# Block 1 of the tokens gathered in place of block 5, with its first rows fetched in the front

## The chip, the cores and the metric

The kernel runs on one core of one Trainium2 chip. The metric is the device time of one execution in microseconds (us), median of several runs. The engines are TensorE (PE; its weight loads are listed apart as PEld), VectorE (DVE), ScalarE (ACT), GpSimd (POOL), and SyncE (SP), which issues plain DMAs. POOL issues the indirect DMAs.

## What is computed

One layer of a streaming encoder on 1024 tokens of width 1024, in float32: an adaptive norm, latent attention and a recurrent branch, merged and projected onto the residual stream; then a second norm and a mixture of 16384 tiny experts. The last part is what the change touches:

```
q = (xt @ w_query).reshape(TOKEN_BLOCK, PEER_HEADS, 2, PEER_HALF)
s = einsum('thpd,hpnd->thpn', q, sub_keys)
s_top, i_top = top_k(s, 16)
cand = s_top[:, :, 0, :, None] + s_top[:, :, 1, None, :]
best, pos = top_k(cand, 16)
idx = ...
g = softmax(best)
act = gelu(einsum('td,thkd->thk', xt, expert_u[idx]))
out = einsum('thk,thkd->td', g * act, expert_v[idx])
```

Each token chooses 8 x 16 = 128 experts out of 16384. An expert is a row of `expert_u` and a row of `expert_v`, of 4 KB each.

## The kernel before

The tokens are eight blocks of 128. The experts of a block are computed in one of two ways. A **gathered** block (`GATHER`, line 23: 0, 5, 6, 7) fetches its own rows: 128 indirect DMAs of 128 rows (512 KB) from `expert_u`, each multiplied with the tokens and summed by one DVE instruction (the dot), then the same number of bytes from `expert_v`, summed by PE with weights from a transposed table. A **dense** block (`DENSE`, the other four: 512 tokens) runs through all experts by matrix products, with a table G that says which of the products count.

The kernel has two halves.

**The front** works through the tokens in two parts of 512 (`part`, line 483): attention, first merge with the projections `ps_ga` and `ps_pa` (`merge_a`), recurrence (`lru`), second merge (`merge_b`), output projection, norm and queries (`ffn_in`, line 839). After part 0's queries, `after_part` (line 1099) puts the expert work of part 0 as a list of small steps into `self.steps`, and while part 1 runs, `pump` (line 137) pops a number of these steps at fixed places. The rates (line 97, second number of each pair: 2 per attention unit, 2.9 per weight product, 6.6 and 3.3 in `ffn_in`) say how many. So the order of the work on each engine is this program order, written out by the counter. What is left over at the end, and part 1's own steps, run behind the last query.

The steps are of four kinds:

- routing of a block (`route`, line 963): DVE picks the 16 best pairs of each head, the weights and the expert numbers. For a gathered block, a further step `turn` transposes the numbers with PE. The routing's tiles `ra`, `rb`, `rc` have one buffer each.
- first rows of a block (`gather_u`, line 1112). In the front it works in rounds of `GUF` = 3: a step `dots` (line 1151) runs three dots on DVE (line 1154) and then issues the next three fetches on POOL (line 1146) into the three buffers that it has just read.
- second rows of block 0 (`sooner_v`, line 1195): a step issues four indirect DMAs of half rows on POOL (line 1209) and lets PE add up the four fetched one step earlier (line 1222). There are 64 row steps, with four buffers of 1024 elements, two for each step.
- the table of a dense block (`table`, line 1263): 32 quads of four tokens, each with two DVE instructions (lines 1294 and 1295), six products on PE (1284, 1286, 1302) and two copies by ACT (1310) into a staging pair `gs`. The pair is written to DRAM after four quads (line 1314); there are two staging buffers, both in use for each four quads.

Before the change, the list of part 0 is block 0's routing, then block 0's rows (first and second) merged evenly with the routing and tables of blocks 1, 2 and 3. Part 1's list is block 4's routing and table, the table merged with the routing of block 5 (`BRIDGE`), whose numbers and weights are kept in constant buffers so that its gathers can begin with the dense stage.

**The dense stage** (`dense`, line 1331) takes the 128 slabs of 128 experts in turn. For each slab: load of `uT` (512 KB, SP) and its split into two fp32r halves by ACT and DVE, 24 matmuls into `ps_A` (`first`), gelu, multiplication with G (`weigh`, from `Gt`, 1 MB for every four slabs), load and split of `expert_v`; after every four slabs, 4 x 2 groups of 12 matmuls into `ps_y` (`second`). A point is 24 matmuls, either of `first` or of one block in `second`; behind each point the same counter pops steps, at a rate of list length over 248 points (128 + 32 x 4, times 0.97). The list of the dense stage is: first rows of block 5 merged with the routings of 6 and 7 and with 40 empty steps; first rows of 6 merged with second rows of 5; first rows of 7 with second rows of 6; second rows of 7. A step there issues one gather (line 1128 for first rows, line 1174 for second rows), runs one dot (line 1134), or adds up four fetched tiles on PE (line 1188).

Of the kernel before, what the change touches and what calls it, by code (L numbers as in the profile page):

```python
# [19 lines left out]
NT = S // T  # L20
EPS = 1e-6
NEG = -3.0e38
GATHER = (0, 5, 6, 7)
SOONER = (0,)
BRIDGE = 5
LATER = (6, 7)
DENSE = tuple(b for b in range(S // 128) if b not in GATHER)
TD = 128 * len(DENSE)
# [56 lines left out]
class Builder:  # L85
    def __init__(self, ctx, tc, I, out, dbg=None, stop=None):
# [6 lines left out]
        self.steps = []  # L93
        self.blocks = {tb: dict(tb=tb) for tb in GATHER}
        self.rate = dict(unit=(1, 2), w=(1.5, 2.9), z=(4, 6.6), q=(2, 3.3))
# [743 lines left out]
    def ffn_in(self, p, ys):  # L839
# [41 lines left out]

        gb = [i for i in range(4) if p * 4 + i in GATHER]

# [79 lines left out]
    def route(self, tb):  # L963

        nc = self.nc
        late = tb in LATER
# [80 lines left out]
        def end():  # L1047
            W2 = t["W"].rearrange("p a b -> p (a b)")
            if f"E{tb}" in self.dbg:
                ee = t["a"]  # L1050
                nc.vector.scalar_tensor_tensor(ee, t["ij"][:, 0, :], 128.0, t["ij"][:, 1, :], op0=ALU.mult, op1=ALU.add)
                self.show(f"E{tb}", ee.rearrange("p (a b) -> p a b", a=8))
                self.show(f"W{tb}", t["W"])
            if tb in GATHER:
                g = self.blocks[tb]
                for n, dt in (("w", F32), ("ei", I32)):
                    g[n] = self.cp.tile([128, 128], dt, name=f"{n}{tb}") if tb == BRIDGE else \
                        (self.gp if late else self.fp).tile([128, 128], dt, tag="g_" + n, bufs=1, name="g_" + n)
                if tb not in SOONER:
                    g["eT"] = self.kept(g, [128, 128], I32, "eT")  # L1060
                nc.vector.tensor_copy(g["w"], W2)
                E = t["ij"][:, 0, :]
                nc.vector.scalar_tensor_tensor(E, E, 128.0, t["ij"][:, 1, :], op0=ALU.mult, op1=ALU.add)
                nc.vector.tensor_copy(g["ei"], E)
                g["E"] = E
            else:
                self.chosen = t["ij"], W2

        def turn():
            g = self.blocks[tb]  # L1070
            pt = self.psum([128, 128], "ps_eT")
            nc.tensor.transpose(pt, g.pop("E"), self.ident)
            if tb in SOONER:
                g["eh"] = [self.fp.tile([128, 128], I32, tag="g_eh", bufs=2, name="g_eh") for _ in range(2)]
                for hf in range(2):
                    nc.vector.tensor_scalar(g["eh"][hf], pt, 2.0, float(hf), op0=ALU.mult, op1=ALU.add)
            else:
                nc.vector.tensor_copy(g["eT"], pt)
# [8 lines left out]
    def kept(self, g, shape, dt, name):  # L1087

        tb = g["tb"]
        if tb in SOONER:  # L1090
            return self.fp.tile(shape, dt, tag="g_" + name, bufs=1, name="g_" + name)
        return self.cp.tile(shape, dt, name=f"{name}{tb}") if name == "eT" and tb == BRIDGE else \
            self.gp.tile(shape, dt, tag="g_" + name, bufs=3 if name == "wT" else 2, name="g_" + name)

    def routed(self, tb):
        st, turn = self.route(tb)
# [2 lines left out]
    def after_part(self, p):  # L1099

        tbs = [tb for tb in range(p * 4, p * 4 + 4) if tb not in LATER]
        tbs = [tb for tb in tbs if tb in GATHER] + [tb for tb in tbs if tb in DENSE]
        rt = {tb: self.soon.pop(tb) if tb in self.soon else self.routed(tb) for tb in tbs}
        dense = sum([rt[tb] + self.table(tb) for tb in tbs if tb in DENSE], [])
        if p == 0:
            self.steps += rt[0] + self.merge(self.gather_u(self.blocks[0]) + self.sooner_v(self.blocks[0]), dense)
        else:
            n = len(rt[4])
            self.steps += dense[:n + 1] + self.merge(dense[n + 1:], rt[BRIDGE])


    def gather_u(self, g):
# [338 lines left out]
    def run(self):  # L1451
# [28 lines left out]
        with (tc.tile_pool(name="dense_b", bufs=1, reuse_waits="tile") as db,  # L1480
              tc.tile_pool(name="dense_a", bufs=1, reuse_waits="tile") as da,
              tc.tile_pool(name="gather", bufs=1, reuse_waits="tile") as self.gp,
              tc.tile_pool(name="pg", bufs=1, space=bass.MemoryType.PSUM, reuse_waits="tile") as self.pg,
              tc.tile_pool(name="psd", bufs=6, space=bass.MemoryType.PSUM, reuse_waits="tile") as self.ps):
            self.fast = 0
            routes = sum([self.routed(tb) for tb in LATER], [])
            us = {tb: self.gather_u(self.blocks[tb]) for tb in GATHER if tb not in SOONER}
            vs = {tb: self.gather_v(self.blocks[tb]) for tb in GATHER if tb not in SOONER}
            idle = [lambda: None]
            self.steps += self.merge(us[5], routes + idle * 40) + self.merge(us[6], vs[5]) + self.merge(us[7], vs[6]) + vs[7]  # L1490
            self.dense(da, db)
            self.pump(1 << 30)

# [54 lines left out]
```

## Time and profile before

| what | value |
|---|---|
| median of 3 runs | 3584.61 us (3577.67 to 3598.39) |
| the profiled execution's own time | 3616.83 us |
| its span, first to last instruction | 3615.1 us |
| mean granted TensorE clock | 0.942 of full speed |
| busy: PE, DVE, POOL, ACT | 3196.5, 2326.8, 1375.2, 1192.0 us |
| moved by DMA | 915.68 MB, 253 GB/s in the mean |

All rows below come from the one profiled execution. A matmul's record begins before the one in front of it has ended, so PE's busy time is the union of its records. The idle time before an instruction is put down to what released it last. Times are counted from the first instruction.

### The profile page before, as it was taken

What the parts mean: (1) busy time and instruction counts of PE and PEld (TensorE: products, weight loads), DVE (VectorE), ACT (ScalarE), POOL (GpSimd) and SP (SyncE); (2) the same over time, 40 slices, a digit from 0 to 9 for tenths busy, and PEclk for the clock granted to TensorE, in tenths of its full rate; (3) what the DMA queues carried; (4) which work ended last, traced back from release to release, by engine and by line L of the source; (5) the groups of instructions that cost most, each with busy time, mean ns of one, the idle gap of its engine ahead of it and who ended that gap; (6) DMA issues with size and microseconds to landing.
All of it is one profiled execution on the core that took longest, in us unless ns stands there. A gap on an engine that the chain in (4) does not pass through costs nothing.

```text
span 3615.1 us, 43218 instructions
## 1 busy us (share of the span) xinstructions
PE 3196.5 (88%) x15408; PEld 2320.3 (64%) x15408; DVE 2326.8 (64%) x5465; ACT 1192.0 (33%) x1860; POOL 1375.2 (38%) x1180
## 2 busy tenths in 40 slices
PE   6899989587878998897697899998989988899997
PEld 4477778465655665565476776665767666666665
DVE  5535557988778644678788776665666565664334
ACT  4437444266425631333332222222222121222121
POOL 0000013134445456431144445555545555554440
PEclk8899999888999999998898999999999999999998
DMA  8422445166776676763788889998999999898995
GB/s 312 161 81 94 135 138 160 58 211 223 265 264 202 230 250 204 242 201 112 247 266 265 288 278 346 340 372 316 351 331 354 344 335 329 312 350 307 346 326 186
DMA packets 392144, 915.68 MB, mean 253 GB/s; under 512 B 162148, under 2 KB 180708, under 8 KB 388088
## 3 DMA queue, kind: packets, MB, share of 16 engines
q0 software_dynamic: 149504, 536.94, 41.9%
q1 hardware_dynamic: 242424, 375.97, 31.9%
q8 instruction: 121, 1.98, 0.2%
q14 instruction: 95, 0.78, 0.1%
HBM read 851.70 MB, written 61.10 MB: 252 GB/s over the span
## 4 chain that ended last, share of the span: by engine, by line
PE 37%; DMA 25%; DVE 19%; issue 11%; ACT 4%; POOL 3%; another core or an unknown queue 0%; SPq 0%; DVEq 0%; POOLq 0%; ACTq 0%
DMA raw<-in_uT 9%; DMA g_u<-in_expert_u,g_ei 5%; DMA raw<-in_expert_v 4%; DVE g_u L1134 3%; PE ps_G L1302 2%; PE ps_y L692 2%; DMA g_u<-in_expert_u,ei 2%; PE ps_y L695 2%; PE g_y L1188 2%; PE ps_y L693 2%; PE h_y L1222 2%; DVE v L105 2%; POOL g_u L1146 2%; PE ps_A L692 1%; PE ps_A L693 1%
## 5 line engine op out<-in xcount | busy, mean ns | idle before, releaser
L1134 DVE CUSTOM_DVE_ANT_0 g_u<-g_u,g_h 128x1024 f32<-128x1024 f32 x384 | 463.9, 1221 | 149.1 <-DMA g_u<-in_expert_u,g_ei 112.2
L692 PE MATMUL ps_A<-dh,u 128*128 128x512 f32 x1024 | 433.3, 423 | 100.6 <-ACT u L104 89.7
L692 PE MATMUL ps_y<-v,w 128*128 128x512 f32 x1024 | 412.9, 403 | 36.2 <-ACT w L104 27.1
L693 PE MATMUL ps_A<-dh,u 128*128 128x512 f32 x1024 | 422.7, 413 | 8.0 <-DMA dh<-d_h2T 8.0
L1128 POOL DMA_INDIRECT g_u<-in_expert_u,g_ei x256 | 298.6, 1167 | 309.3 <-issue 100.8
L693 PE MATMUL ps_y<-v,w 128*128 128x512 f32 x1024 | 404.6, 395 | 0.0
L1174 POOL DMA_INDIRECT g_v<-in_expert_v,g_eT x256 | 284.8, 1112 | 255.0 <-PE g_y L1188 101.4
L1209 POOL DMA_INDIRECT h_v<-in_expert_v,g_eh x256 | 273.6, 1069 | 283.1 <-PE h_y L1222 212.8
L105 DVE TENSOR_TENSOR u<-raw,u 128x1024 fp32r<-128x1024 f32 x128 | 156.7, 1224 | 326.9 <-ACT u L104 308.9
L104 ACT CAST u<-raw 128x1024 fp32r<-128x1024 f32 x128 | 134.0, 1047 | 659.7 <-DMA raw<-in_uT 620.3
L692 PEld LDWEIGHTS ps_A<-dh,u 128*128 128x128 f32 x1024 | 206.9, 202 | 198.0 <-ACT u L104 110.9
L1128 POOL DMA_INDIRECT g_u<-in_expert_u,ei x128 | 163.2, 1275 | 341.9 <-DVE oneA L1295 103.7
L104 ACT CAST v<-raw 128x1024 fp32r<-128x1024 f32 x128 | 134.3, 1049 | 451.7 <-PE ps_y L695 252.4
L695 PE MATMUL ps_y<-v,w 128*128 128x512 f32 x1024 | 279.7, 394 | 0.3 <-DVE w L105 0.3
L692 PEld LDWEIGHTS ps_y<-v,w 128*128 128x128 f32 x1024 | 195.2, 191 | 124.4 <-issue 36.9
L105 POOL TENSOR_TENSOR whl<-wraw,whl 128x1024 fp32r<-128x1024 f32 x16 | 40.6, 2539 | 585.5 <-ACT whl L104 585.4
L1146 POOL DMA_INDIRECT g_u<-in_expert_u,g_ei x128 | 152.6, 1192 | 282.4 <-DVE g_act L1154 116.3
L695 PE MATMUL ps_A<-dh,u 128*128 128x512 f32 x1024 | 253.1, 389 | 0.8 <-DVE u L105 0.8
L104 ACT CAST whl<-wraw 128x1024 fp32r<-128x1024 f32 (+2 forms) x152 | 151.1, 995 | 297.1 <-PE ps_pb L695 55.2
L693 PEld LDWEIGHTS ps_A<-dh,u 128*128 128x128 f32 x1024 | 206.9, 202 | 52.8 <-DMA dh<-d_h2T 9.0
L105 DVE TENSOR_TENSOR whl<-wraw,whl 128x1024 fp32r<-128x1024 f32 (+2 forms) x136 | 155.2, 1142 | 116.1 <-ACT whl L104 112.7
L695 PEld LDWEIGHTS ps_y<-v,w 128*128 128x128 f32 x1024 | 194.6, 190 | 46.3 <-DVE w L105 4.0
(375 smaller groups left out, 6818.7 us busy)
## 6 DMA issues: line engine op xcount, KB each, us to landing
raw<-in_uT SPq DMA_DIRECT2D x128, 512.0 KB
raw<-in_expert_v SPq DMA_DIRECT2D x128, 512.0 KB
wraw<-in_w_in SPq DMA_DIRECT2D x64, 512.0 KB
d_G<-gs SPq DMA_DIRECT2D x64, 512.0 KB
Gt<-d_G SPq DMA_DIRECT2D x32, 1024.0 KB
wada<-in_w_ada SPq DMA_DIRECT2D x32, 512.0 KB
wraw<-in_w_query SPq DMA_DIRECT2D x32, 512.0 KB
x<-in_x SPq DMA_DIRECT2D x16, 512.0 KB
```

What stands on the lines that cost most here:

```text
L104: self.nc.scalar.copy(hi, src)
L105: (eng or self.nc.vector).tensor_tensor(lo, src, b32(hi), op=ALU.subtract)
L692: nc.tensor.matmul(ps, lh, rh, start=(n == 0), stop=False)
L693: nc.tensor.matmul(ps, lh, rl, start=False, stop=False)
L695: st = nc.tensor.matmul(ps, ll, rh, start=False, stop=(n == len(terms) - 1))
L1128: st = nc.gpsimd.indirect_dma_start(out=u[:], out_offset=None, in_=I["expert_u"], in_offset=bass.IndirectOffsetOnAxis(ap=g["ei"][:, s:s + ...
L1134: nc.vector.tensor_tensor_reduce(out=u, in0=u, in1=g["h2"], scale=1.0, scalar=0.0, op0=ALU.mult, op1=ALU.add, accum_out=g["act"][:, s:s + 1])
L1146: fetch = lambda s: [nc.gpsimd.indirect_dma_start(out=us.setdefault(k, gp.tile([128, 1024], F32, tag="gu", bufs=GUN, name="g_u"))[:], out_ ...
L1174: st = nc.gpsimd.indirect_dma_start(out=v[:], out_offset=None, in_=I["expert_v"], in_offset=bass.IndirectOffsetOnAxis(ap=g["eT"][:, t:t + ...
L1188: nc.tensor.matmul(g["y"][q * 32:(q + 1) * 32, hf * 512:(hf + 1) * 512], zs[n // 16][:, q, (r % 4) * 32:(r % 4 + 1) * 32], v4[q][:, hf * 5 ...
L1209: nc.gpsimd.indirect_dma_start(out=v[:, m, :], out_offset=None, in_=halves, in_offset=bass.IndirectOffsetOnAxis(ap=g["eh"][hf][:, tok:tok ...
L1222: nc.tensor.matmul(t["y"][q * 32:(q + 1) * 32, :], z[:, q, :], v[q // 2][:, q % 2, :], start=(r == 0), stop=(r == 31), tile_position=(0, q ...
```

## The change

Block 1 becomes a gathered block and block 5 a dense one. Block 1 is in part 0, so its routing and its first rows go into part 0's list, behind block 0's second rows; they use block 0's buffers and rounds of three. Its transposed numbers and weights are kept in constant buffers, and its second rows are fetched in the dense stage, merged with the first rows of block 6. The tables of part 0 are now those of blocks 2 and 3; behind the last queries come the tables of blocks 4 and 5. In the dense stage the routings of blocks 6 and 7 stand alone, each ahead of its block's first rows, and the first rows of block 5 with their 40 empty steps fall away. Rates and buffer counts stay.

```diff
--- before.py
+++ after.py
@@ -20,9 +20,8 @@
 NT = S // T
 EPS = 1e-6
 NEG = -3.0e38
-GATHER = (0, 5, 6, 7)
-SOONER = (0,)
-BRIDGE = 5
+GATHER = (0, 1, 6, 7)
+SOONER = (0, 1)
 LATER = (6, 7)
 DENSE = tuple(b for b in range(S // 128) if b not in GATHER)
 TD = 128 * len(DENSE)
@@ -1054,9 +1053,8 @@
             if tb in GATHER:
                 g = self.blocks[tb]
                 for n, dt in (("w", F32), ("ei", I32)):
-                    g[n] = self.cp.tile([128, 128], dt, name=f"{n}{tb}") if tb == BRIDGE else \
-                        (self.gp if late else self.fp).tile([128, 128], dt, tag="g_" + n, bufs=1, name="g_" + n)
-                if tb not in SOONER:
+                    g[n] = (self.gp if late else self.fp).tile([128, 128], dt, tag="g_" + n, bufs=1, name="g_" + n)
+                if tb:
                     g["eT"] = self.kept(g, [128, 128], I32, "eT")
                 nc.vector.tensor_copy(g["w"], W2)
                 E = t["ij"][:, 0, :]
@@ -1070,7 +1068,7 @@
             g = self.blocks[tb]
             pt = self.psum([128, 128], "ps_eT")
             nc.tensor.transpose(pt, g.pop("E"), self.ident)
-            if tb in SOONER:
+            if tb == 0:
                 g["eh"] = [self.fp.tile([128, 128], I32, tag="g_eh", bufs=2, name="g_eh") for _ in range(2)]
                 for hf in range(2):
                     nc.vector.tensor_scalar(g["eh"][hf], pt, 2.0, float(hf), op0=ALU.mult, op1=ALU.add)
@@ -1087,10 +1085,9 @@
     def kept(self, g, shape, dt, name):
 
         tb = g["tb"]
-        if tb in SOONER:
+        if tb == 0:
             return self.fp.tile(shape, dt, tag="g_" + name, bufs=1, name="g_" + name)
-        return self.cp.tile(shape, dt, name=f"{name}{tb}") if name == "eT" and tb == BRIDGE else \
-            self.gp.tile(shape, dt, tag="g_" + name, bufs=3 if name == "wT" else 2, name="g_" + name)
+        return self.cp.tile(shape, dt, name=f"{name}{tb}") if tb in SOONER else self.gp.tile(shape, dt, tag="g_" + name, bufs=3 if name == "wT" else 2, name="g_" + name)
 
     def routed(self, tb):
         st, turn = self.route(tb)
@@ -1101,12 +1098,14 @@
         tbs = [tb for tb in range(p * 4, p * 4 + 4) if tb not in LATER]
         tbs = [tb for tb in tbs if tb in GATHER] + [tb for tb in tbs if tb in DENSE]
         rt = {tb: self.soon.pop(tb) if tb in self.soon else self.routed(tb) for tb in tbs}
-        dense = sum([rt[tb] + self.table(tb) for tb in tbs if tb in DENSE], [])
+        dense = [rt[tb] + self.table(tb) for tb in tbs if tb in DENSE]
         if p == 0:
-            self.steps += rt[0] + self.merge(self.gather_u(self.blocks[0]) + self.sooner_v(self.blocks[0]), dense)
+            g = self.blocks
+            self.steps += rt[0] + self.merge(self.gather_u(g[0]) + self.sooner_v(g[0]) + rt[1] + self.gather_u(g[1]),
+                                             sum(dense, []))
         else:
             n = len(rt[4])
-            self.steps += dense[:n + 1] + self.merge(dense[n + 1:], rt[BRIDGE])
+            self.steps += rt[4] + self.merge(dense[0][n:], rt[5]) + dense[1][len(rt[5]):]
 
 
     def gather_u(self, g):
@@ -1483,11 +1482,9 @@
               tc.tile_pool(name="pg", bufs=1, space=bass.MemoryType.PSUM, reuse_waits="tile") as self.pg,
               tc.tile_pool(name="psd", bufs=6, space=bass.MemoryType.PSUM, reuse_waits="tile") as self.ps):
             self.fast = 0
-            routes = sum([self.routed(tb) for tb in LATER], [])
-            us = {tb: self.gather_u(self.blocks[tb]) for tb in GATHER if tb not in SOONER}
-            vs = {tb: self.gather_v(self.blocks[tb]) for tb in GATHER if tb not in SOONER}
-            idle = [lambda: None]
-            self.steps += self.merge(us[5], routes + idle * 40) + self.merge(us[6], vs[5]) + self.merge(us[7], vs[6]) + vs[7]
+            us = {tb: self.gather_u(self.blocks[tb]) for tb in LATER}
+            vs = {tb: self.gather_v(self.blocks[tb]) for tb in GATHER if tb}
+            self.steps += self.routed(6) + self.merge(us[6], vs[1]) + self.routed(7) + self.merge(us[7], vs[6]) + vs[7]
             self.dense(da, db)
             self.pump(1 << 30)
```

## Rows read from the trace of the kernel before

**Rows 1.** The page, part 1: busy us, share of the span, instructions.

```profile
PE 3196.5 (88%) x15408; PEld 2320.3 (64%) x15408; DVE 2326.8 (64%) x5465; ACT 1192.0 (33%) x1860; POOL 1375.2 (38%) x1180
```

**Rows 2.** Windows by stage: start:end, us, engines' busy us, PE clock, DMA share, GB/s.

```profile
core 0: us, PE busy (x) PEld busy (x) DVE busy (x) ACT busy (x) POOL busy (x), PEclk, DMA share, GB/s
728.00:932.00 204.00, 175.44 (x982) 123.74 (x981) 167.71 (x457) 132.54 (x279) 82.42 (x71) 0.90 0.70 227
932.00:1055.00 123.00, 102.45 (x457) 76.95 (x456) 87.65 (x143) 35.89 (x59) 49.18 (x42) 0.90 0.79 270
1055.00:1220.00 165.00, 140.22 (x609) 93.98 (x608) 131.01 (x359) 90.09 (x115) 82.21 (x71) 0.95 0.66 215
1220.00:1375.00 155.00, 152.93 (x771) 99.71 (x770) 77.06 (x138) 65.07 (x98) 82.51 (x80) 1.00 0.77 255
1375.00:1522.00 147.00, 128.27 (x736) 83.78 (x735) 79.44 (x186) 34.55 (x53) 80.27 (x75) 0.94 0.68 220
1522.00:1667.00 145.00, 141.06 (x781) 101.42 (x780) 116.63 (x561) 51.37 (x88) 48.81 (x48) 0.99 0.57 190
1667.00:1760.00 93.00, 58.86 (x325) 38.62 (x323) 85.78 (x280) 34.67 (x70) 0.94 (x1) 0.80 0.31 114
1760.00:2165.00 405.00, 340.29 (x1390) 272.73 (x1391) 325.44 (x614) 105.85 (x135) 162.31 (x127) 0.92 0.87 279
2165.00:3265.00 1100.00, 1006.93 (x4651) 725.06 (x4650) 678.05 (x1010) 240.67 (x307) 602.18 (x512) 0.96 0.95 339
3265.00:3545.00 280.00, 279.12 (x1425) 183.04 (x1424) 102.02 (x134) 60.33 (x77) 131.70 (x128) 1.00 0.94 333
3545.00:3615.00 70.00, 49.57 (x224) 38.95 (x223) 30.48 (x34) 8.90 (x12) 0.00 (x0) 0.87 0.40 133
```

**Rows 3.** Waits, 2165 to 3265 us: engine line <- releaser: us, times, longest.

```profile
ACT u L104 <- DMA raw<-in_uT: 417.8, 64, 22.0
```

**Rows 4.** Tile g_u, 727 to 1103 us: ns min/median/max, first and last start.

```profile
L1146 POOL DMA_INDIRECT g_u<-in_expert_u,g_ei x128: 932/938/2462, 727.2 to 1095.0; - x128
L1154 DVE CUSTOM_DVE_ANT_0 g_u<-g_u,g_h x128: 1204/1224/1274, 732.6 to 1100.9; 128x1024 f32<-128x1024 f32 x128
```

**Rows 5.** Timeline of DVE, 1059 to 1085 us: start, us, engine, line, operation [idle].

```profile
1059.39 1.22 DVE L1154 CUSTOM_DVE_ANT_0 g_u<-g_u,g_h 128x1024 f32<-128x1024 f32 x1
...
1065.45 1.23 DVE L1154 CUSTOM_DVE_ANT_0 g_u<-g_u,g_h 128x1024 f32<-128x1024 f32 x1 [2.74 <-DMA g_u<-in_expert_u,g_ei]
...
1067.83 1.22 DVE L1154 CUSTOM_DVE_ANT_0 g_u<-g_u,g_h 128x1024 f32<-128x1024 f32 x1
...
1075.35 1.21 DVE L1154 CUSTOM_DVE_ANT_0 g_u<-g_u,g_h 128x1024 f32<-128x1024 f32 x1
...
1082.04 1.21 DVE L1154 CUSTOM_DVE_ANT_0 g_u<-g_u,g_h 128x1024 f32<-128x1024 f32 x1
```

**Rows 6.** The page's part 5 for block 0's second rows; tile h_v's idle; one window.

```profile
L1209 POOL DMA_INDIRECT h_v<-in_expert_v,g_eh x256 | 273.6, 1069 | 283.1 <-PE h_y L1222 212.8
...
  issue: 30.8, 101
...
1350.00:1400.00 50.00, 47.83 (x262) 30.25 (x261) 22.57 (x45) 10.20 (x14) 33.63 (x33) 1.00 0.76 240
```

**Rows 7.** Lines of DVE, 1690 to 1760 us: the table's two instructions.

```profile
L1295 DVE SCALAR_TENSOR_TENSOR oneA<-ps_d,ch 128x512 f32<-128x512 f32 x32 | 21.9, 683 | 3.5 <-PE ps_d L1286 3.3
L1294 DVE TENSOR_TENSOR oneB<-cst,ch 128x512 f32<-128x512 f32 x32 | 21.7, 678 | 0.0
```

**Rows 8.** Timeline of ACT, 1690 to 1760 us: the copies out of the table's products.

```profile
1706.17 1.03 ACT L1310 COPY gs<-ps_G 128x256 f32<-128x256 f32 x2 [2.31 <-DMA d_G<-gs]
...
1712.78 1.04 ACT L1310 COPY gs<-ps_G 128x256 f32<-128x256 f32 x2 [2.30 <-DMA d_G<-gs]
```

**Rows 9.** Windows of the gathered sums' matmuls on PE (tile g_y).

```profile
2165.00:3265.00 1100.00, 124.86 (x1008) 0.96 0.95 339
3265.00:3545.00 280.00, 66.62 (x512) 1.00 0.94 333
```

## The prediction

> **What bounds the kernel now.** I began with part 1 of the page [rows 1]: PE is busy 88% of the span, but no engine is full throughout, so the bound has to be read by stage. I therefore cut the span into windows, from the start of part 1's attention onward [rows 2]. Everything earlier is the same work after the change. Four things are to be seen there. (i) From 728 to 1667 us, the projections of tokens 512 to 1023 run on PE (85 to 99% busy from 1055 on), and block 0's gathers are mixed in by a counter of steps. (ii) From 1667 to 1760 us, behind the last query, the front's remaining steps run alone: DVE is busy 86 of 93 us, DMA 31%. (iii) The dense stage starts at 1760 us. From 2165 to 3265 us its DMA share is 0.95 at 339 GB/s, while PE has 93 us idle; ACT there waits 418 us for the next table slab [rows 3]. That is DMA-bound. (iv) From 3265 us PE is full. So the change takes bytes from a stage that lacks DMA time, and puts them, with their DVE work, into stages with a fifth to two fifths of their DMA time free.
>
> **How the front's gathers run.** In program order each pump runs so many steps, and DVE, POOL and PE keep this order. A gather round of the front is three POOL fetches into three buffers, then three dot products on DVE; the next fetch goes out only when its buffer's dot is done. All 128 dots took 732.6 to 1100.9 us [rows 4], 43 rounds at 8.6 us. The timeline shows rounds starting at 1059.39, 1067.83, 1075.35 and 1082.04 us, and DVE standing idle for a landing inside them [rows 5]: 8.4, 7.5 and 6.7 us. I take 7.1, the mean of the last two; bounds 6.7 and 8.6. A step of block 0's second rows issues four gathers at 1.07 us (273.6 us for 256) with 0.30 us between [rows 6], so 5.5 us at least. The densest slice holds 33 issues in 50 us, 6.1 us a step [rows 6], which I take; the stage from 1220 to 1375 us, paced partly by the counter, holds 80 issues in 155 us, 7.7, the upper bound.
>
> **The change, part by part.** *Counting steps.* Part 1's pumps are 70 in the attention, 34.8 in the first merge, 52.2 in the recurrence, 46.4 in the second merge, 26.4 in the output projection and 56.1 in the queries, 285.9 in all, and they do not change. The list does: 279 steps before (24, 14 and 5 rounds of block 0 in the first three stages, then 15, 19, 11 and 20 second-row steps), 290 after. The same pumps then get 38 rounds in the attention; 5 rounds and 15 second-row steps in the first merge; 33 second-row steps in the recurrence; 17 in the second merge, with block 1's routing behind them; 7 rounds of block 1 in the output projection; 35 rounds in the queries; 4 steps left over. One fewer table is in the list.
>
> *Attention* (204 us, 71 fetches issued [rows 2], so nearly 23 rounds done). 37 rounds at 7.1 us are 263 us: **+59** (+44 to +114). DVE alone would not force it: 14 more rounds of 3.7 us, less 14 table steps of 1.36 us (two instructions of 0.68 us [rows 7]), add 33 us to 168 of 204. The softmax is queued behind each waiting dot on DVE, and PE waits for it.
>
> *First merge* (123 us): 6 rounds and 15 steps, 43 + 92 = 135: **+12** (0 to +21). *Recurrence* (165 us): 33 × 6.1 = 201: **+36** (+17 to +89); the steps' matmuls stand in PE's queue, so the weights' matmuls behind them wait for the gather. *Second merge* (155 us): 17 × 6.1 = 104 us, and 18 of 46.4 pumps with no gather at about 2 us of PE each (16 products of 24 matmuls, at the 0.248 us derived below, over 46.4 pumps), 35 us: **−16** (−26 to +11). *Output projection and norm* (147 us): 7 rounds are 50 us, hidden beside PE's 128 us: **0** (±15).
>
> *Queries* (145 us). 35 rounds at 7.1 us are 249 us: **+104**. DVE's own floor: 117 us busy, less 8 table steps (11 us), plus 35 × 3.7 = 128, is 234: +89 at least; at 8.6 us a round, +156. PE's cover of 141 us is gone here: DVE and the landing of rows become the bound. *Left over*: one round, two table steps, the act's end: **+8** (0 to +15).
>
> *A second table behind the queries.* Block 5's routing already runs there, mixed with block 4's table, so only the 36 table steps are new, with nothing beside them. ACT's copies into the staging pair come in groups of four quads; the group at 1706.17 us and the one at 1712.78 us each begin when the previous pair has been written out [rows 8]: 6.6 us a group, 8 groups and a start of 4 us: **+56**. Bounds: 44 us (DVE's 32 × 1.36) and 68 us (the first table's whole length there, 1690 to 1758). Its 16 stores join SP's queue, and the dense stage's first factors wait for them.
>
> *Costed at nothing:* block 1's row store of h2 and two DVE operations on 128x1024 elements move from part 1 to part 0, four transposed stores the other way; SP's count stays equal, and PE and DVE of both query stages hide them while they last. The retired buffer for block 5's indices costs nothing in time.
>
> *Front in all:* 59 + 12 + 36 − 16 + 0 + 104 + 8 + 56 = **+259** (+173 with each term at its low end).
>
> *Dense stage.* A point is 24 matmuls; there are 256. Matmul records without the gathered sums' [rows 2, 9] give 57.9 points from 1760 to 2165 us (7.0 us each), 151.8 to 3265 (7.25) and 38.0 to 3545 (7.4). The last two windows' PE busy times, two equations, give 0.248 us a matmul and 0.103 us a gathered-sum record; the first window then comes out at 345 us, and the row says 340. After: 693 steps in place of 866 on 248 points, 2.79 a point instead of 3.49. Routing takes 10 points: 10 × 7.0 and 20 us of start, 90 us. Two merged pairs of lists (266 steps each) take 190.6 points. Their DMA need is 512 gathers and 0.66 MB a point of slabs and factors: 394 MB, 1163 us at 339 GB/s; PE's is 4574 × 0.248 + 1024 × 0.103 = 1240 us, or 6.5 a point. Both are near each other, so neither is reached: I take 6.8, nearest the first window's 7.0 (DMA 0.87 there), 1296 us. The last rows take 47.7 points at 7.05 us, 336; the end is unchanged at 70. Sum 1792 against 1855: **−63** (−120 at 6.5 us a point, −25 at 7.0). The 156 us of dots that leave DVE buy nothing: it was busy 678 of 1100 us.
>
> **Sum:** 259 − 63 = +196 us. The profiled execution took 3616.83 us, 0.9% over the median of 3584.61; put on the median, 3780 us.
>
> A rule on the price of a gather: rows show 0.94 us for an issue at the median [rows 4] and rounds of 6.7 to 8.4 us [rows 5]. The Trainium skill (DMA: Bandwidth & Descriptors, "Anatomy of one DMA — SWDGE") fits 2.0 us plus bytes over 436 GB/s; for 512 KB an estimate from it is 3.2 us, a round 5.6 us, and the sum would be about +77, 3662 us. No run here shows that pace. A rule that speaks against the change: the row shows an issue lasting from 0.93 to 2.46 us while dots run [rows 4]. The Trainium skill (GPSIMD Engine Reference, "Key points") says GpSimd shares its SBUF interfaces with VectorE and contends with instructions of two SBUF inputs, as the dots are; denser dots would then push rounds to the upper bound.
>
> **The rivals.**
> 1. *Rounds pace the front* (the forecast), chance 0.62: 3780 us.
> 2. *Rounds run at the low bounds*, since fewer table steps stand between the dots; the queries then sit on DVE's floor: 44 + 0 + 17 − 26 + 89 + 8 + 56 = +188, less 63: 3710 us. For it: the 6.7 us round. Against: a mean of 8.6. Chance 0.17. The fit named above would put this case lower still.
> 3. *Rounds stay at 8.6 us*, since DMA is fuller everywhere: 114 + 21 + 36 − 16 + 156 + 8 + 68 = +387, less 25: 3947 us. Chance 0.12.
> 4. *The other side: the dense stage gives back all its waiting.* Place: 2165 to 3265 us, where the DMA is the only full resource. Its price: down to PE's need, 6144 × 0.248 + 1536 × 0.103 = 1682 us, −173. It decides from the point where the front's growth stays under 155 us; with the low bounds and the DVE floor of the queries partly hidden in the stretch behind them (+140), 3552 us. Against: the first window, with DMA at 0.87, still lost 65 us of PE. Chance 0.06.
> 5. *The change does not do what it says:* block 1's routing shares single buffers with block 3's, starts late, and its rounds slide behind the queries, beside the two tables. DVE's 258 us there replace the 149 of the tables, the queries shrink to 134: again near 3765 us. Chance 0.03.
>
> **How the numbers follow.** 0.5%, 18 us, is what a measurement of this kernel can tell from no change. Cases 1, 2, 3 and 5 are slower by far more; of case 2's chance 0.02 is for rounds so short that the sum falls within 18 us, and 0.01 beyond; case 4 is faster but for 0.01. So faster 0.06, same 0.03, slower 0.91. The range runs from 3640 us (case 2 with the dense gain at its high end, 3653, and a little more) to 3900 (rounds at 8.1 us, so 78 more for the 78 rounds, and the dense gain at its low end, 38 more); outside it remain case 4, the low tail of case 2 and the upper half of case 3.
>
> **What would show it.** Right: 128 more fetches on the front's line; dots of block 0 ending before about 1070 us; the attention some 60 us longer with DVE idle for landings; the queries near 250 us with DVE over 90% busy and PE near 55%; about 150 us between the last query and the first dense matmul; dense points near 6.8 us, DMA share near 0.9. Wrong: rounds of 6 us or less, a query stage under 200 us, or a dense stage under 1730 us.

## The result, and the profile after

The changed kernel takes **3790.65 us** (median of 3 runs, 3783.28 to 3794.2) against 3584.61 us before: ratio **1.057**, 95% interval 1.0533 to 1.0606, so 206 us more. The profiled execution took 3794.2 us (span 3792.4 us, mean TensorE clock 0.917 of full speed).

Part 1 of the page after the change, to set beside [rows 1], and two lines of its part 5: the front's fetches, now 256, and their dots.

```profile
PE 3258.9 (86%) x15408; PEld 2358.7 (62%) x15408; DVE 2332.5 (62%) x5465; ACT 1194.6 (32%) x1863; POOL 1316.3 (35%) x1180
...
L1145 POOL DMA_INDIRECT g_u<-in_expert_u,g_ei x256 | 283.0, 1106 | 555.2 <-DVE g_act L1153 202.5
...
L1153 DVE CUSTOM_DVE_ANT_0 g_u<-g_u,g_h 128x1024 f32<-128x1024 f32 x256 | 311.3, 1220 | 144.2 <-DMA g_u<-in_expert_u,g_ei 143.1
```

The instruction counts are nearly those of before; the front's 256 dots now wait 143 us for landings, where the 128 of before waited 65. (Line numbers are one or two lower than before.) The windows by stage, columns as in [rows 2]: attention, first merge, recurrence, second merge, output projection and norm, queries, the stretch behind them, the dense stage to the end, and two windows inside the dense stage.

```profile
728.00:997.00 269.00, 191.77 (x872) 133.36 (x873) 205.24 (x531) 123.64 (x258) 111.90 (x108) 0.75 0.74 235
997.00:1147.00 150.00, 117.81 (x537) 75.90 (x536) 82.75 (x232) 38.51 (x58) 83.43 (x81) 0.89 0.76 252
1147.00:1353.00 206.00, 196.58 (x886) 113.67 (x884) 91.23 (x189) 108.41 (x142) 132.53 (x129) 0.98 0.76 249
1353.00:1479.00 126.00, 120.84 (x482) 68.77 (x478) 56.88 (x130) 23.84 (x33) 70.11 (x68) 1.00 0.69 215
1479.00:1592.00 113.00, 73.79 (x519) 65.57 (x519) 90.80 (x195) 29.15 (x46) 30.14 (x28) 0.80 0.63 211
1592.00:1875.00 283.00, 174.75 (x721) 134.64 (x719) 236.45 (x790) 56.12 (x95) 108.13 (x91) 0.76 0.68 226
1875.00:2038.00 163.00, 117.87 (x654) 77.80 (x655) 137.81 (x337) 67.82 (x135) 10.63 (x10) 0.79 0.51 184
2038.00:3792.00 1754.00, 1641.27 (x7685) 1205.57 (x7684) 988.00 (x1530) 416.43 (x532) 717.56 (x640) 0.97 0.87 294
...
2120.00:2720.00 600.00, 567.84 (x2648) 418.98 (x2647) 363.82 (x530) 144.30 (x184) 272.99 (x238) 0.98 0.92 313
2780.00:3400.00 620.00, 581.97 (x2699) 429.90 (x2698) 370.47 (x540) 142.78 (x181) 278.02 (x246) 0.98 0.90 306
```

These stages begin at the first matmul of each stage's own products (`ps_ga`, `ps_g`, `ps_pb`, `ps_z`, `ps_qr`; the last `ps_sc`; the first `ps_A`), which is not quite where I cut [rows 2]. Cut at the same marks in every trace, the lengths in us are:

| stage | before | dense alone | after | short dots | no rows of 1 | four buffers | control (run 7) | before, four |
|---|---|---|---|---|---|---|---|---|
| attention | 209 | 209 | 269 | 183 | 270 | 287 | 267 | 230 |
| first merge | 119 | 113 | 150 | 193 | 149 | 118 | 153 | 112 |
| recurrence | 194 | 189 | 206 | 208 | 202 | 184 | 205 | 174 |
| second merge | 128 | 129 | 126 | 126 | 127 | 120 | 134 | 122 |
| projection, norm | 111 | 100 | 113 | 105 | 85 | 132 | 113 | 113 |
| queries | 177 | 176 | 283 | 204 | 144 | 247 | 283 | 162 |
| behind them | 93 | 98 | 163 | 172 | 144 | 148 | 166 | 94 |
| dense, to last `ps_y` | 1834 | 1760 | 1735 | 1733 | 1735 | 1745 | 1751 | 1832 |

Where the time came from is read on DVE. Tile g_u in the two stretches in which block 0's and block 1's rows are fetched (columns as in [rows 4]; the last line of each is the time from a fetch's issue to its landing):

```profile
L1145 POOL DMA_INDIRECT g_u<-in_expert_u,g_ei x128: 932/937/3070, 731.4 to 1049.1; - x128
L1153 DVE CUSTOM_DVE_ANT_0 g_u<-g_u,g_h x128: 1197/1225/1257, 737.0 to 1054.9; 128x1024 f32<-128x1024 f32 x128
...
DMA to landing us min/median/max: 4.1/5.2/11.7
...
L1153 DVE CUSTOM_DVE_ANT_0 g_u<-g_u,g_h x128: 1197/1220/1262, 1519.2 to 1903.5; 128x1024 f32<-128x1024 f32 x128
...
DMA to landing us min/median/max: 4.1/5.4/9.8
```

Block 0's rows come at (1054.9 - 737.0) / 127 = 2.50 us each, 7.5 us a round of three, where before they took 8.6 [rows 4]; block 1's at 3.03 us, 9.1 us a round. The waits of the attention (728 to 997 us), of the queries (1592 to 1875) and of most of the dense stage (2120 to 3400), columns as in [rows 3]:

```profile
DVE g_u L1153 <- DMA g_u<-in_expert_u,g_ei: 55.4, 65, 4.8
ACT P L666 <- DVE sm L664: 49.1, 23, 6.1
PE ps_pT L592 <- ACT P L666: 36.8, 17, 6.3
...
PE ps_G L1301 <- DVE oneA L1294: 90.0, 14, 9.3
DVE g_u L1153 <- DMA g_u<-in_expert_u,g_ei: 44.5, 31, 4.4
PE ps_qr L694 <- DVE whl L104: 18.1, 3, 11.9
...
ACT u L103 <- DMA raw<-in_uT: 539.3, 92, 18.8
```

The sum to read: in the attention DVE is busy 205 us and stands 55 us before a dot whose rows have not landed, 260 of 269 us. In the queries it is 236 + 45 = 281 of 283 us. So nearly all of DVE's idle time is that one wait, and DVE's queue is the length of both stages. What PE needs from DVE (the softmax's sums by way of ACT, the one-hot tables `oneA`, the split of the query weights) stands behind the dots, and PE is idle 77 and 108 us.

The same two stages before, cut at the same marks, with the attention's wait:

```profile
728.00:937.00 209.00, 180.09 (x1011) 127.08 (x1010) 171.89 (x464) 134.17 (x282) 83.83 (x72) 0.90 0.70 228
DVE g_u L1154 <- DMA g_u<-in_expert_u,g_ei: 27.3, 24, 5.0
...
1490.00:1667.00 177.00, 171.03 (x924) 121.67 (x924) 141.41 (x622) 63.88 (x109) 61.05 (x60) 0.99 0.61 204
```

In the attention DVE already filled 172 + 27 = 199 of 209 us, so only 10 us were free. In the queries DVE was busy 141 of 177 us with no rows to wait for, and PE, busy 171 us, was the longer queue.

### The profile page after: what moved, and what is told of

It reads as the page before. It is cut to its first block, busy times and chain, and to the rows that moved or that the text cites. A ratio compares the mean times of both kernels' runs of the same rounds, so it can differ in the third digit from the quotient of the medians.

```text
span 3792.4 us, 43185 instructions
## 1 busy us (share of the span) xinstructions
PE 3258.9 (86%) x15408; PEld 2358.7 (62%) x15408; DVE 2332.5 (62%) x5465; ACT 1194.6 (32%) x1863; POOL 1316.3 (35%) x1180
## 4 chain that ended last, share of the span: by engine, by line
issue 13%; PE 12%; DMA 11%; POOL 7%; DVE 6%; ACT 1%; POOLq 0%; DVEq 0%; ACTq 0%; SPq 0%
DMA raw<-in_uT 6%; POOL g_v L1173 4%; POOL g_u L1127 3%; DMA raw<-in_expert_v 2%; DMA g_u<-in_expert_u,g_ei 2%; PE ps_G L1301 2%; PE ps_y L691 2%; PE ps_y L694 2%; PE ps_y L692 2%; PE g_y L1187 1%; PE ps_A L691 1%; PE ps_A L692 1%; DVE g_u L1133 1%; DVE yac L1410 1%; PE ps_A L694 1%
## 5 line engine op out<-in xcount | busy, mean ns | idle before, releaser
L1145 POOL DMA_INDIRECT g_u<-in_expert_u,g_ei x256 | 283.0, 1106 | 555.2 <-DVE g_act L1153 202.5
L691 PE MATMUL ps_A<-dh,u 128*128 128x512 f32 x1024 | 419.8, 410 | 53.1 <-ACT u L103 52.9
L1127 POOL DMA_INDIRECT g_u<-in_expert_u,g_ei x256 | 287.0, 1121 | 395.7 <-PE ps_A L694 165.3
L692 PE MATMUL ps_A<-dh,u 128*128 128x512 f32 x1024 | 411.7, 402 | 0.0
L1153 DVE CUSTOM_DVE_ANT_0 g_u<-g_u,g_h 128x1024 f32<-128x1024 f32 x256 | 311.3, 1220 | 144.2 <-DMA g_u<-in_expert_u,g_ei 143.1
L1133 DVE CUSTOM_DVE_ANT_0 g_u<-g_u,g_h 128x1024 f32<-128x1024 f32 x256 | 311.0, 1221 | 142.2 <-DMA g_u<-in_expert_u,g_ei 142.1
L1208 POOL DMA_INDIRECT h_v<-in_expert_v,g_eh x256 | 263.8, 1031 | 132.6 <-PE h_y L1221 65.1
L691 PEld LDWEIGHTS ps_A<-dh,u 128*128 128x128 f32 x1024 | 199.9, 195 | 141.7 <-ACT u L103 69.5
L691 PEld LDWEIGHTS ps_y<-v,w 128*128 128x128 f32 x1024 | 195.2, 191 | 118.5 <-issue 36.9
L1301 PE MATMUL ps_G<-oneA,oneB 128*128 128x128 f32 x1024 | 168.7, 315 | 113.8 <-DVE oneA L1294 113.4
L1173 POOL DMA_INDIRECT g_v<-in_expert_v,eT x128 | 148.6, 1161 | 315.3 <-PE ps_A L694 217.1
L694 PE MATMUL ps_A<-dh,u 128*128 128x512 f32 x1024 | 252.9, 389 | 0.0
L1301 PEld LDWEIGHTS ps_G<-oneA,oneB 128*128 128x128 f32 x1024 | 147.5, 219 | 147.8 <-issue 96.6
```

Source lines behind the costliest of these rows:

```text
L691: nc.tensor.matmul(ps, lh, rh, start=(n == 0), stop=False)
L692: nc.tensor.matmul(ps, lh, rl, start=False, stop=False)
L694: st = nc.tensor.matmul(ps, ll, rh, start=False, stop=(n == len(terms) - 1))
L1127: st = nc.gpsimd.indirect_dma_start(out=u[:], out_offset=None, in_=I["expert_u"], in_offset=bass.IndirectOffsetOnAxis(ap=g["ei"][:, s:s + ...
L1133: nc.vector.tensor_tensor_reduce(out=u, in0=u, in1=g["h2"], scale=1.0, scalar=0.0, op0=ALU.mult, op1=ALU.add, accum_out=g["act"][:, s:s + 1])
L1145: fetch = lambda s: [nc.gpsimd.indirect_dma_start(out=us.setdefault(k, gp.tile([128, 1024], F32, tag="gu", bufs=GUN, name="g_u"))[:], out_ ...
```

## The experiments

Each kernel was compared with the kernel before, run beside it; edits are to the changed kernel unless said otherwise. The changed kernel itself was not run again beside them, and the median of the kernel before moved between 3584.61 and 3594.73 us, so differences from 3790.65 us are uncertain by some 10 us.

**1. Short dots.** The front's dots read 64 of the 1024 elements, so the activations of blocks 0 and 1 are sums of 64 terms.

```diff
-  tensor_tensor_reduce(out=u, in0=u, in1=g["h2"], ...
+  tensor_tensor_reduce(out=u[:, 0:64], in0=u[:, 0:64], in1=g["h2"][:, 0:64], ...
```

> The changed kernel with the front's dots over 64 of 1024 columns, so the output is not the reference's; all fetches stay. Theory (a round is a loop of dot, issue and landing over three buffers): a round loses one dot of its loop, 7.2 to about 6.0 us; attention 269 to about 222, queries 283 to about 240, in all 95 us less, about 3695 us, and DVE waits longer for landings. Rival A (DVE's work alone sets these stages): they fall back to about 206 and 177 us, 166 us or more less, 3625 us or below. Rival B (the bytes set them): under 20 us less, above 3770 us.

Measured: 3678.99 us, ratio 1.0243 (1.0175 to 1.0311), 112 us less than the changed kernel. Tile g_u of this kernel for both blocks:

```profile
L1153 DVE CUSTOM_DVE_ANT_0 g_u<-g_u,g_h x128: 204/225/234, 737.5 to 1013.9; 128x64 f32<-128x64 f32 x128
...
DMA to landing us min/median/max: 4.0/5.3/11.4
...
L1153 DVE CUSTOM_DVE_ANT_0 g_u<-g_u,g_h x128: 201/224/228, 1478.4 to 1794.8; 128x64 f32<-128x64 f32 x128
```

A round still takes (1013.9 - 737.5) / 127 × 3 = 6.5 us for block 0 and 7.5 for block 1, with dots of 0.22 us. So a landing of 5.3 us at the median and a turn on the queue remain, whatever DVE computes: both the landing and DVE's work are in the round. The query stage follows the same sum. Its window, and the wait in it (1542 to 1745 us):

```profile
1542.00:1745.00 203.00, 154.88 (x720) 120.53 (x720) 143.74 (x766) 55.59 (x94) 84.83 (x80) 0.84 0.86 289
```

```profile
DVE g_u L1153 <- DMA g_u<-in_expert_u,g_ei: 50.2, 35, 5.8
...
PE ps_gw L1140 <- DVE g_act L1138: 69.7, 1, 69.7
```

144 + 50 = 194 of 203 us; I had expected about 240. The last line is of the first merge (911 to 1104 us): the attention fell to 183 us, lower than I had expected, but the first merge grew to 193. There the transpose of block 0's activations (`ps_gw`) stands in PE's queue and waits 70 us for the last dots; in the changed kernel it waits 21.5 us, and the trace of the kernel before shows no such wait. So part of the attention's gain was only moved.

The edit did more than shorten the dots. The list of steps is the same, but the order on DVE in the trace is not: 74 dots stand ahead of the attention's last softmax sum, where the changed kernel has 101 (runs 2, 3 and 7 too). The attention and the queries hold 78 and 80 dots in place of 106 and 92, so dots left both stages for later ones. The stage lengths therefore do not show what shorter dots alone would give; the pace of the rounds does. It also means that the order on an engine is not the counter's alone, as my account of the kernel before has it. What else sets it is not known.

**2. The second table.** First attempt: its steps left out, and its stores made a second time out of the table of block 2, so block 5's table is left out.

```diff
-  self.steps += rt[4] + self.merge(dense[0][n:], rt[5]) + dense[1][len(rt[5]):]
+  self.steps += rt[4] + self.merge(dense[0][n:], rt[5])
...
+  if tb == 2: nc.sync.dma_start(self.d_G[c + 24, ...], t["st"][m])
```

> The changed kernel without block 5's table: its factors are block 2's, stored a second time in the front, so the output is not the reference's. Theory (the second table behind the queries stands alone, paced by its staging pair and DVE): 44 to 68 us less than the changed kernel, so about 3730 us, and the stretch from the last query to the first dense matmul falls from 163 to about 105 us. Rival (that stretch waits for block 1's last rounds anyway, so the table is half hidden): under 25 us less, above 3765 us.

Measured: 3772.72 us, ratio 1.0501 (1.0439 to 1.0562), only 18 us less. The stretch behind the queries did shrink, from 163 to 118 us; but the stages from the attention to the second merge took 24 us longer and the dense stage 16, in one trace. Whether the moved stores did that is not shown, since fronts with the same work differ by some 20 us between executions (run 4), so this attempt does not price the table. Second attempt, without them: the dense stage reads block 2's part of the table in place of block 5's.

```diff
-  self.steps += rt[4] + self.merge(dense[0][n:], rt[5]) + dense[1][len(rt[5]):]
+  self.steps += rt[4] + self.merge(dense[0][n:], rt[5])
...
-  nc.sync.dma_start(Gs[g]..., self.d_G[:, :, lo:hi, :]...)
+  for a, b, n in ((0, 0, 24), (24, 0, 8)):
+      nc.sync.dma_start(Gs[g][:, a:a + n]..., self.d_G[b:b + n, :, lo:hi, :]...)
```

> The changed kernel without block 5's table, with no store added: the dense stage reads block 2's factors for block 5 (two loads for each four slabs in place of one, the same bytes), so the output is not the reference's. Theory (the second table costs what its stretch showed): about 46 us less than the changed kernel, near 3745 us, with the stretch from the last query to the first dense matmul near 117 us and all else within 10 us. Rival (the table is half hidden): under 25 us less, above 3765 us.

Measured: 3753.66 us, ratio 1.0473 (1.0424 to 1.0523), 37 us less. The one stage that changes is the stretch behind the queries, now 120 us:

```profile
1870.00:1990.00 120.00, 65.94 (x334) 43.34 (x333) 96.59 (x273) 39.30 (x75) 10.83 (x11) 0.68 0.42 153
```

The table costs 43 us there, where I had expected 46. In the changed kernel the second table stands alone from 1986 to 2038 us (first line; the second is the last wait before the dense stage in this run, without the table):

```profile
1986.00:2038.00 52.00, 52.00 (x317) 35.15 (x316) 41.03 (x63) 30.69 (x61) 0.00 (x0) 0.96 0.75 265
...
PE ps_A L691 <- DMA dh<-d_h2T: 10.0, 1, 10.0
```

PE is busy throughout and DVE 41 of the 52 us. The 32 quads follow each other every 1.62 us, while a quad's two DVE instructions take 1.36; DVE waits for PE's `ps_d` before 24 of them. So here PE's order, and not DVE, is the longer queue. Without the table the first dense matmul waits 10 us for its load, which the table had covered: 52 less 10 is about the 43.

**3. No rows of block 1 in the front.** Its rounds are empty steps, its weights a constant, so its activations are left out.

```diff
-  ... + rt[1] + self.gather_u(g[1]),
+  ... + rt[1] + self.no_rows(g[1]),   # 45 empty steps, then memset of wT to 0.01
```

> The changed kernel with empty steps in place of block 1's first rows (no fetches, no dots; its weights are a constant, so the output is not the reference's). Theory (rounds of block 1 pace the queries): the query stage, first to last product, falls from 283 to about 177 us and the leftover by 8, so 115 us less, about 3675 us; the attention keeps its 269 us, since block 0's rounds still come at the denser pace. Rival (the query stage is long because PE's clock fell or the stores of h2 moved): it stays above 230 us, and the time above 3730 us.

Measured: 3603.6 us, ratio 1.0026 (0.9992 to 1.006), 187 us less than the changed kernel. The queries and the stretch behind them:

```profile
1562.00:1706.00 144.00, 138.00 (x722) 110.72 (x721) 129.54 (x606) 55.01 (x93) 0.00 (x0) 0.98 0.35 117
1706.00:1850.00 144.00, 116.35 (x653) 77.21 (x653) 123.86 (x311) 67.60 (x138) 0.00 (x0) 0.85 0.46 171
```

The same 720 matmuls take 138 us of PE at a clock of 0.98, where beside the rounds they took 175 at 0.76. The rows cost more than I had expected of them: the query stage without them takes 144 us, not the 177 of before, which still carried second rows of block 0. By stage they cost 139 us in the queries, 28 in projection and norm, 19 behind.

**4. The dense stage's new order alone,** made in the kernel before: block 5's first rows are left out (its weights a constant), and the list is the new one.

```diff
-  self.steps += self.merge(us[5], routes + idle * 40) + self.merge(us[6], vs[5]) + self.merge(us[7], vs[6]) + vs[7]
+  self.steps += [ones] + self.routed(6) + self.merge(us[6], vs[5]) + self.routed(7) + self.merge(us[7], vs[6]) + vs[7]
```

> The kernel before with the changed kernel's dense list alone: block 5's first rows are neither fetched nor multiplied, its weights are a constant, so the output is not the reference's; the front is untouched. Theory (the dense stage is short of DMA time and gives back part of the 67 MB): 63 us less by the forecast, 101 by the trace after, so 3485 to 3520 us, with the front's 1760 us unchanged. Rival (the dense gain came from where the changed front leaves buffers and tables): under 40 us less, above 3545 us. Rival (all waiting goes): 150 us or more less, below 3435 us.

Measured: 3518.42 us, ratio 0.9781 (0.9719 to 0.9843), 72 us less than before. Its dense stage to the end, and below it the kernel before's:

```profile
1742.00:3522.00 1780.00, 1651.91 (x7684) 1210.50 (x7684) 991.11 (x1533) 414.79 (x529) 719.64 (x640) 0.97 0.86 293
```

```profile
1760.00:3615.00 1855.00, 1675.91 (x7685) 1219.78 (x7685) 1136.00 (x1790) 415.75 (x530) 896.20 (x767) 0.95 0.91 317
```

DMA share falls from 0.91 to 0.86, and PE's idle time from 179 to 128 us. How much of the gain is the bytes and how much the new order, the run does not part. Its front is the one of before and ends at 1742 us, not 1760: a front's length differs by some 20 us between two executions.

**5. The exchange of blocks without the front's rows,** made in the kernel before: block 1 is gathered, block 5 dense with its table behind the queries, but block 1's first rows stay in the dense stage.

```diff
-GATHER = (0, 5, 6, 7)
+GATHER = (0, 1, 6, 7)
-BRIDGE = 5
+BRIDGE = 1
...
-  rt[0] + self.merge(... self.sooner_v(self.blocks[0]), dense)
+  rt[0] + self.merge(... self.sooner_v(self.blocks[0]), rt[1] + [lambda: None] * 36 + sum(dense, []))
-  dense[:n + 1] + self.merge(dense[n + 1:], rt[BRIDGE])
+  rt[4] + self.merge(dense[0][n:], rt[5]) + dense[1][len(rt[5]):]
-  self.merge(us[5], routes + idle * 40) + self.merge(us[6], vs[5]) + ...
+  self.merge(us[1], routes + idle * 40) + self.merge(us[6], vs[1]) + ...
```

> Block 1 gathered in place of block 5 as in the change, with two tables behind the queries, but its first rows fetched in the dense stage, in the list of the kernel before; empty steps stand for its table in the front, so that block 0's pace is that of before. Theory (the first rows in the front cost the time, the exchange of blocks only the second table): the kernel before plus 46 us, less up to 20 us for the table that leaves the front: 3610 to 3645 us, the query stage near 175 us, the dense stage as before. Rival (the exchange of blocks itself is dear): above 3680 us.

Measured: 3619.49 us, ratio 1.0075 (1.0038 to 1.0111), 30 us over the runs of before beside it (3589.95 us). So some 30 of the 206 us belong to the exchange and its table; the rest, some 170 (3790.65 - 3619.49), is the move of block 1's first rows into the front, the dense stage's gain already taken off. The total came as expected, the stages did not: in its trace the attention takes 193 us, the first merge 93, the queries 205 (about 175 expected) and the stretch behind them 150. Why the queries took 205 us with the work of before (61 fetches and 923 matmul records, against 60 and 924 in the 177 us) is open; the mean granted clock there was 0.93, against 0.99.

**6. and 7. Four fetch buffers, and their control.** Rounds of four in place of three; the room is found by taking two small buffers of the pool `front_a`. The control takes the two buffers only. Rounds of four also shorten each block's list by 11 steps, so the counter runs further ahead.

```diff
-GUF = 3
+GUF = 4
...
-tc.tile_pool(name="front_a", bufs=9, reuse_waits="tile") as fa,
+tc.tile_pool(name="front_a", bufs=7, reuse_waits="tile") as fa,
```

> The changed kernel with rounds of four fetches into four buffers; the front's small-tile tags have seven buffers in place of nine to make room (the next kernel has the seven alone). Theory (a round waits for its landing): four rows per loop of little more length, attention down by 20 to 40 us and queries by 25 to 45 against the seven buffers alone, in all 50 to 80 us less. Rival (DVE's work sets these stages): under 20 us between the two.

> The changed kernel with seven buffers in place of nine for each of the front's small-tile tags, as a control for four buffers. Both theories: within 30 us of the changed kernel, 3780 to 3820 us, since PE's products run ahead a little less.

Measured: 3722.58 us, ratio 1.0364 (1.0316 to 1.0411); control 3806.92 us, ratio 1.0592 (1.0544 to 1.064), whose interval holds the changed kernel's ratio. Four buffers give 84 us. Block 0's dots, with four buffers and in the control:

```profile
L1153 DVE CUSTOM_DVE_ANT_0 g_u<-g_u,g_h x128: 1172/1224/1271, 734.9 to 998.9; 128x1024 f32<-128x1024 f32 x128
```

```profile
L1153 DVE CUSTOM_DVE_ANT_0 g_u<-g_u,g_h x128: 1200/1224/1256, 738.4 to 1053.7; 128x1024 f32<-128x1024 f32 x128
```

2.08 us a row against 2.48, at the same price of a dot; block 1's rows come at 2.63 us against 3.03. DVE's waits for landings fall from 70.0 to 36.8 us for block 0's rows and from 68.4 to 53.2 for block 1's, 48 of the 84 us: the loop from a buffer's fetch to its next one did hold the rows. What the shorter list adds is not parted from it. By stage I was wrong on the attention: it is 19 us longer than the control's, not 20 to 40 shorter, for all 128 dots of block 0 now fall in it (105 in the control). The two merges, the recurrence and the queries are 14 to 36 us shorter, the projection 19 longer.

**8. Four buffers in the kernel before** (same edit).

> The kernel before with rounds of four fetches into four buffers and seven buffers of each small-tile tag. Theory (a round waits for its landing, and before the change PE covers part of it): block 0's rows need about 2.4 us each in place of 2.9, attention and first merge 10 to 40 us shorter, in all 10 to 30 us less than before: 3560 to 3580 us, a version faster than both kernels. Rival (the seven small tiles cost what the rounds give, as PE runs ahead less): 3585 us or more.

Measured: 3582.24 us, ratio **0.9953** (0.993 to 0.9976): 12 us less than the kernel before beside it, a little faster than both kernels and 2 us above the range that I had expected. Block 0's rows come at 2.54 us, not 2.4 (2.90 before). The merges, the recurrence and the queries are 6 to 20 us shorter, but the attention, which I had expected to be shorter, is 21 us longer.

**9. Fewer steps in the attention,** in the kernel before.

```diff
-self.rate = dict(unit=(1, 2), w=(1.5, 2.9), z=(4, 6.6), q=(2, 3.3))
+self.rate = dict(unit=(1, 1.6), w=(1.5, 3.2), z=(4, 6.6), q=(2, 3.3))
```

> The kernel before with 1.6 steps per attention unit in place of 2, and 3.2 per weight product in place of 2.9, so that 19 in place of 24 rounds fall into the attention. Theory (each waiting dot holds the softmax on DVE): attention 209 to about 190 us, merges 10 us longer, in all 0 to 20 us less than before. Rival (the attention is not held by the rounds): attention unchanged within 5 us, total 0 to 15 us more.

Measured: 3602.44 us, ratio 1.0014 (0.9992 to 1.0035). The attention fell from 209 to 173 us, more than expected, and the total stayed: the first merge, the recurrence and the second merge took back 32 us (130, 199 and 144 us against 119, 194 and 128). A step put elsewhere takes its time there.

## Why the prediction was right, point by point

**The time.** 3780 us forecast, 3790.65 measured; the first case, rounds that pace the front, is what happened. That the total came within 11 us is partly luck: the front's growth and the dense stage's gain were both forecast too small, by like amounts, and cancel. To its last `ps_y` the dense stage took 1733 to 1751 us in six traces with the new list (after, and runs 1, 2 in its second attempt, 3, 6 and 7; mean 1739) and 1820 to 1834 in three with the old one (before, runs 8 and 9; mean 1829): a gain of 90 us (86 with run 2's first attempt, 1751, and run 5, 1822), or of 72 by run 4's medians, not 63. By the medians the front then grew by 278 to 296 us, not 259. (In the two profiled executions alone it is 278 and 101; the one of before was 32 us over its median.) With each term at its low end the forecast's front is +153, not the +173 that stands there; neither the range nor the chances use that figure. Means of before and run 4 (both with the old front) and of after and run 7 (the new one) give the stages:

- **Attention:** +59, as forecast, by two errors that cancel: its rounds ran at 7.5 us, not 7.1, but 35 of them fall in it, not 37. DVE's idle time for landings and the end of block 0's dots before 1070 us came as named.
- **First merge, recurrence, second merge:** +35, +14 and +1 against +12, +36 and -16. My windows of [rows 2] end elsewhere, so only the three together can be judged: +50 against +32. What the sum left out is the wait of 21.5 us of `ps_gw` behind block 0's last dots, with the first merge's products queued behind it on PE.
- **Output projection and norm:** +7 against 0 (±15).
- **Queries:** +106 against +104, by luck, for three steps were off. The rounds took 9.2 us (92 dots in 283 us), beyond the upper bound of 8.6, since DVE's top-16 work stands between the dots; and 31 of them fell there, not 35. My window also began 32 us after the stage's first product, so its 145 us of before are 177. DVE's busy time was forecast at 234 us and is 236, over a stage 32 us longer and with 4 rounds fewer than the forecast's; and I said over 90% busy and PE near 55%, and it is 84% and 62%: the landing waits come on top of the work, not beside it.
- **Left over and second table:** +69 against 8 + 56. The table itself takes 52 us, 6.5 us for four quads, so the 6.6 us a group of [rows 8] was the right pace, but it is PE's order that sets it, not the staging pair. Only 43 us of it lengthen the stretch (run 2, second attempt), just under the lower bound of 44, because it covers a wait of 10 us that would stand there without it. What is left over costs some 19 us (run 3) to 26 (69 - 43), not 8: the last of 11 dots of block 1 ends 30 us after the last `ps_sc`. The stretch behind the queries is 163 us, near the 150 named.
- **Dense stage:** the pace came as forecast. From 2120 to 2720 us 2648 matmul records, less 496 of the gathered sums, are 89.7 points in 600 us, **6.7 us a point**; from 2780 to 3400 us 91.1 points (2699 records less 512) take 6.8; I had said 6.8. PE is idle 6% of these windows, against 8% from 2165 to 3265 us before; DMA share 0.92 and 0.90. ACT's waits for slabs, 539 us in 1280, did not fall at all (418 in 1100, [rows 3]), so they do not measure what the stage loses to the DMA, as I had read them. By the sums' first matmuls (2085 and 3414 us) the start and block 6's routing took 47 us against 55 (half of the 70 for two routings, and 20), the two merged pairs with block 7's routing 1329 against 1331, the last rows (to 3727 us) 313 against 336, the end 65 against 70. The step that was off is the last rows' pace of 7.05 us; and the 1855 us from which the sum was taken were about 5 us long (1834 against the mean of 1829).

**The rivals.** Rounds at low bounds (3710 us) would need 6.7 us in the mean; with three buffers only short dots reach it. Rounds held at 8.6 us are true of block 1 (9.1) and not of block 0 (7.5). The rival on the other side, in which the dense stage gives back all its waiting, fails by its price: 72 to 90 us of 173, against a front that grew by well over 155. The last, in which block 1's rounds slide behind the queries, did not come either: 117 of its 128 dots ran before the last query product, and the queries took 283 us, not 134.

**The two rules of the Trainium skill.** A fetch lands 5.2 us after its issue at the median, 4.1 at the least. The estimate from the Trainium skill (DMA: Bandwidth & Descriptors, "Anatomy of one DMA — SWDGE") was 3.2 us; this chip's trace does not agree, with up to three fetches and the stage's loads under way at once. On the sharing of SBUF interfaces by GpSimd and VectorE (the Trainium skill, GPSIMD Engine Reference, "Key points") the runs say little: with dots cut from 1.22 to 0.22 us the median issue stays at 0.94 us, and the mean falls from 1.106 to 1.021 us, in a kernel whose order changed too.

## What to carry to other kernels

Work that is put "beside" a stage with a fixed engine order is free only if the queue that it shares has room: add up, for each in-order engine, its busy time and the time it will stand before data that has not landed, and if that sum passes the stage's length, the sum is the new length. A gather through few buffers is a loop (issue, landing, use, next issue): here 5.2 + 1.2 us and a turn on the queue for three rows, and a fourth buffer, with its shorter list, was worth 84 us, a use of 0.2 us, with its other order, 112. And the same bytes can be cheap in one stage and dear in another: block 1's 128 first rows made the front 187 us longer, where a block's first rows had cost the dense stage 72 to 90.

## What the runs showed that I had not expected

**PE's clock was lower where PE waited.** From the attention to the first dense matmul PE has the same products and is busy 993 us against 899 (windows of the kernel after, then before):

```profile
728.00:2038.00 1310.00, 993.40 (x4660) 669.69 (x4661) 901.16 (x2399) 447.48 (x763) 546.87 (x512) 0.84 0.69 227
```

```profile
728.00:1760.00 1032.00, 899.24 (x4652) 618.20 (x4650) 745.27 (x2119) 444.18 (x760) 426.33 (x385) 0.93 0.66 218
```

In the stages held by DVE the mean granted clock is 0.75 and 0.76, a mixture of the two levels of 1.2 and 2.4 GHz, where before it was 0.90 and 0.99; PE was busy 71% and 62% of them, where before it was 86% and 97%. How much of these 94 us lies on the path is open, since DVE's sum accounts for both stages already.

**Moved stores.** 16 more stores of 512 KB in the front (run 2, first attempt) went with 24 us there, in one trace; that they caused it is not shown.
